# First stage of a hybrid decoder step: latents, rotary keys and p turned in 32x32 blocks on VectorE and stored in pieces of 128 bytes

## The chip, the cores and the metric

The kernel runs on one core of one Trainium2 chip. The metric is the device time of one execution in microseconds, the median of several runs. Beside the timed runs there is one profiled execution, from which the trace and the profile page come. In names of engines, PE is TensorE, DVE is VectorE, ACT is ScalarE, POOL is GpSimd and SP is SyncE, which issues nearly all DMAs here.

## The reference

One layer of a decoder with two token mixers side by side, on 1024 prompt tokens and on 8 sequences of 4 sampled tokens (32 rows). What matters here is the head of the layer and what it hands to later stages:

```python
z = rmsnorm(x, ln_w) @ w_in
rq, rk, rv, rg, cq, ckv, kr, mg, ga, gb = jnp.split(z, ...)   # cq 384, ckv 256, kr 64 columns
q = (rmsnorm(cq, q_norm_w) @ w_uq)...
ckv = rmsnorm(ckv, kv_norm_w)
kr = rope(kr, pos)
...
sc = einsum('bqhd,bkhd->bhqk', qn, k_nope) + einsum('bqhr,bkr->bhqk', qr, kr)   # MLA scores of the prompt
...
x = x + sigmoid(x @ w_ple_gate) * (p @ w_ple_proj)            # p: 256 columns per token
```

The 384 + 256 + 64 = 704 columns of cq, ckv and kr are called the latents here (NLAT). They are computed with tokens on the 128 partitions, while the matmuls that use them later need columns on the partitions and tokens along the free dimension. The same holds for p and for x. Turning them is what this document is about.

## The kernel before, in words

All matrix products of the prompt are done in three passes of float32r parts (a high and a low part of each operand), by `mac` (lines 266 to 268): three matmuls for one product. `stage` (line 240) loads a piece of a weight, POOL or ACT makes its high part (line 196 or 247) and DVE its low part (line 199, `lo_of`).

The first stage (`latents`, line 461) goes over nine tiles of tokens in the order 0, 1, 8, 2 to 7; tile 8 is the 32 sampled rows. For each it issues, in program order: `turn_tile` of the tile two places ahead (DMA of x into `xt` long before; eight TensorE transposes at line 323 into two PSUM banks, copies to `turn`, a store to the scratch `xTD`); `latent_tile` (48 matmuls with the resident weights `wlat`, two norms, the rotation of the keys by `rope_nat`, stores of ckv and of the rotary keys to the outputs and of the keys to the scratch `krD`); then, one tile later, the turn of the tile's latents: three transposes at line 404, two at line 406, copies by ACT (line 408) and DVE (line 409) into `lt`, one store to the scratch `latD` (line 410); `scale_tile` of the tile two places ahead (a transposed scale by line 350, then `xn` by lines 353 to 359); and `turn_p` (line 329), which loads 256 columns of p into `pl`, turns them by two transposes (line 323), copies them by ACT and stores them to `pTD` (line 325). All transposes of the first stage use the PSUM tag `tr`, three banks.

`beside` (line 485) lets matmuls of the gates (`fill`, their stores at line 422) run between the last three tiles. Program order is a priority; within it the tile framework orders each engine's instructions by when they come ready in its own model, and puts in all waits. Every engine, and SP's queue of DMA issues too, then runs in the order so fixed. The SBUF pool of the first stage (`p1`) is closed behind it (line 486). The pool of the next stage (`p3`) takes the same memory: its first loads (`early`, lines 526 and 529, weights of the sample queries, used at line 538) can only be issued when the last tile of `p1` has been read.

Much later, in the retention's last head (lines 1078 to 1082), the latents and the rotary keys are loaded back: `latD` row by row into five tiles, `krD` as `krN`, with tokens on the partitions. At the start of the MLA stage `rope_keys` (line 1126) turns the keys by eight transposes (line 1131) and makes `krA` and `krB`, high and low parts, each with its 64 rows twice, for the score matmuls at lines 1261 and 1262. `embedding` (line 1471) loads `pTD` near the end.

Of the kernel before, what the change touches and what calls it, by code (L numbers as in the profile page):

```python
# [9 lines left out]
F32 = mybir.dt.float32  # L10
# [9 lines left out]
P = 128  # L20
D = 1024
SEQ = 1024
# [3 lines left out]
NT = SEQ + NR  # L26
TH = NT // 3
# [8 lines left out]
ROPE = 64  # L36
QL = 384
KL = 256
PLE = 256
# [5 lines left out]
NLAT = QL + KL + ROPE  # L45
# [116 lines left out]
def decode_step(ctx: ExitStack, tc: tile.TileContext, A: dict, O: dict):  # L162
    nc = tc.nc
    pe, act, dve, pool, sp = nc.tensor, nc.scalar, nc.vector, nc.gpsimd, nc.sync
# [3 lines left out]
    dram = ctx.enter_context(tc.tile_pool(name="scratch", bufs=1, space=DRAM))  # L168
# [11 lines left out]
    def tr():  # L180
        return banks["pool"].tile([P, 512], F32, tag="tr", name="tr", bufs=3)
# [10 lines left out]
    def b32(ap):  # L192
        return ap.bitcast(F32)
# [4 lines left out]
    def lo_of(out, src, hi):  # L198
        dve.tensor_tensor(out=out, in0=src, in1=b32(hi), op=ALU.subtract)  # L199
# [9 lines left out]
    ident = C("ident")  # L209
# [7 lines left out]
    gbD = [dram.tile([P, NT], F32, tag=f"gb{f}", name=f"gb{f}") for f in range(8)]  # L217
    mgD = [dram.tile([P, NT], F32, tag=f"mg{f}", name=f"mg{f}") for f in range(8)]
    gtD, goD = ([dram.tile([P, 4, NT], F32, tag=f"{n}{h}", name=f"{n}{h}") for h in range(HR)] for n in ("gt", "go"))
    latD = dram.tile([P, 5, SEQ], F32, tag="latD", name="latD")  # L220
    xTD = dram.tile([P, 8, NT], F32, tag="xTD", name="xTD")
    pTD = dram.tile([P, 2, NT], F32, tag="pTD", name="pTD")
    krD = dram.tile([P, 8, ROPE], F32, tag="krD", name="krD")

    w_in = A["w_in"][0]

# [59 lines left out]
    p1 = ph.enter_context(tc.tile_pool(name="p1", bufs=2))  # L286
# [27 lines left out]
    def turn_input(t, src, dst, nf, by=act.copy):  # L314

        n = rows(t)
        turned = []
        for half in range(0, nf, 4):
            st = p1.tile([P, 4, P], F32, tag="turn", name="turn", bufs=4)
            w = min(4, nf - half)  # L320
            pt = tr()
            for i in range(w):
                pe.transpose(pt[:, i * P:i * P + n], src[:n, (half + i) * P:(half + i + 1) * P], ident[:n, :n])
            by(st[:, :w, :n], pt[:, :w * P].rearrange("p (a b) -> p a b", a=w)[:, :, :n])
            sp.dma_start(dst[:, half:half + w, t * P:t * P + n], st[:, :w, :n])
            turned.append(st)
        return turned

    def turn_p(t):
        n = rows(t)  # L330
        pl = p1.tile([P, PLE], F32, tag="pl", name="pl", bufs=2)
        sp.dma_start(pl[:n], A["p_prompt"][0, 0, t * P:(t + 1) * P, :] if t < 8 else A["p_sample"].rearrange("l b t c -> (l b t) c"))
        turn_input(t, pl, pTD, PLE // P)

    turned = {}

# [44 lines left out]
    def latent_tile(t):  # L381
        n = rows(t)
        pq, pk = ac(), ac()
        for ps, lo, w in ((pq, 0, QL), (pk, QL, KL + ROPE)):
            for k in range(8):
                xk = tuple(v[:, t * P:t * P + n] for v in xn[k])
                wk = tuple(v[:, lo:lo + w] for v in wlat[k])
                mac(ps[:n, :w], xk, wk, k == 0, k == 7)
        la = latS if t == 8 else p1.tile([P, NLAT], F32, tag="la", name="la", bufs=2)
        cq, kv, kr = la[:n, 0:QL], la[:n, QL:QL + KL], la[:n, QL + KL:NLAT].unsqueeze(1)  # L390
        for src, dst, w, nw in ((pq[:n, :QL], cq, QL, qnw), (pk[:n, :KL], kv, KL, kvw)):
            ss = small(p1, "ss2")
            act.activation(dst, src, AF.Square, accum_out=ss[:n])
            r = rstd_of(p1, ss, n, 1.0 / w)
            dve.scalar_tensor_tensor(out=dst, in0=src, scalar=r[:n], in1=nw[:n], op0=ALU.mult, op1=ALU.mult)
        rope_nat(kr, pk[:n, KL:KL + ROPE].unsqueeze(1), t, n, p1, 1, "kro")
        if t < 8:
            sp.dma_start(O["ckv_prompt"][0, 0, t * P:(t + 1) * P, :], kv)
            sp.dma_start(O["krope_prompt"][0, 0, t * P:(t + 1) * P, :], la[:, QL + KL:])
            sp.dma_start(krD[:, t, :], la[:, QL + KL:])  # L400
            yield
            pt, pt2 = tr(), tr()
            for i in range(3):
                pe.transpose(pt[:, i * P:(i + 1) * P], la[:, i * P:(i + 1) * P], ident)
            for i in range(2):
                pe.transpose(pt2[:, i * P:(i + 1) * P], la[:, (3 + i) * P:(4 + i) * P], ident)
            lt = p1.tile([P, 5, P], F32, tag="lt", name="lt", bufs=2)
            act.copy(lt[:, 0:3, :], pt[:, :3 * P].rearrange("p (a b) -> p a b", a=3))
            dve.tensor_copy(lt[:, 3:5, :], pt2[:, :2 * P].rearrange("p (a b) -> p a b", a=2))
            sp.dma_start(latD[:, :, t * P:(t + 1) * P], lt)  # L410
        else:
            sp.dma_start(O["ckv_sample"].rearrange("l b t c -> (l b t) c"), kv)
            sp.dma_start(O["krope_sample"].rearrange("l b t c -> (l b t) c"), la[:n, QL + KL:])
# [365 lines left out]
    qkA, qkB = slots(qk8, "qkA", 4), slots(qk8, "qkB", 4)  # L779
# [288 lines left out]
    for h in range(HR):  # L1068
        chunks = prompt_chunks(h, X)
        for cost in chunks:  # L1070
            if cost is None:
                break
        nxt = {}
        if h + 1 < HR:
            rest = (head_in(h + 1, nxt), 50.3)
        else:
            rest = (gate_tiles(C_MG, mgD, range(5, 8), AF.Silu), 31.8)
            raws = [(qkB if i < 4 else qkA)("lat", (P, SEQ), F32) for i in range(5)]
            for i, raw in enumerate(raws):
                sp.dma_start(raw, latD[:, i, :])  # L1080
            krN = qkA("krN", (P, 8, ROPE), F32)
            sp.dma_start(krN, krD)
        run(woven((chain(chunks, sample_state(h, X)), 27.9 if h + 1 < HR else 32.4), rest))
        X = nxt
    hi_by[0] = hi_pool
# [18 lines left out]
    def split(raw, hi, lo):  # L1104
        act.copy(hi, raw)
        lo_of(lo, raw, hi)
        return hi, lo
# [17 lines left out]

    def rope_keys():
        for u in range(2):
            pt = tr()
            us = slice(u * 512, (u + 1) * 512)
            for i in range(4):  # L1130
                pe.transpose(pt[:ROPE, i * P:(i + 1) * P], krN[:, 4 * u + i, :], ident)
            act.copy(krA[0:ROPE, us], pt[:ROPE])
            act.copy(krA[ROPE:P, us], pt[:ROPE])
            lo_of(krB[0:ROPE, us], pt[:ROPE], krA[0:ROPE, us])
            act.copy(krB[ROPE:P, us], b32(krB[0:ROPE, us]))
            yield 0.43

    HB = 4

# [331 lines left out]
    def embedding(j):  # L1471
        pT = [xs_("pT", (P, 2, TH)) for _ in range(2)]
        for k in range(2):
            hi, lo = (pT[k][:, i, :] for i in range(2))
            raw = xs_("pTr", (P, TH), F32)
            sp.dma_start(raw, pTD[:, k, j * TH:(j + 1) * TH])
            split(raw, hi, lo)
        return pT

# [136 lines left out]
```

## Time and profile before

| | us |
|---|---|
| median of 3 runs | 2175.15 (2174.05 to 2175.59) |
| the profiled execution's own time | 2167.49 |
| its span in the trace | 2165.7 |
| TensorE busy | 2125.3 (98%) |
| VectorE busy | 1249.4 (58%) |
| ScalarE busy | 726.9 (34%) |
| GpSimd busy | 326.4 (15%) |

The granted TensorE clock of the profiled execution is 0.998 of full speed. Line numbers in rows (L404) are those of the kernel. A row of a group reads: line, engine, operation, output <- inputs, shapes, count | busy time in us (overlaps counted once), mean ns of one | idle time of the engine just before them and what ended it. A row of the timeline reads: start and duration in us, engine, line, operation, tile names, count of merged instructions, and in brackets the idle time before it and its releaser. SPq is SP's queue of DMA issues: its durations are those of the issue, not of the transfer. A row of a tile reads: line, engine, operation, count, shortest, median and longest ns, first and last start in us. A row of waits reads: who waited, for whom, us in total, times, longest us. Rows of q1 are the DMA queue that SP feeds: packets, MB, and the time that the packets took as a share of 16 engines in that window.

### The profile page before, as it was taken

The numbers are of one execution on the slowest core, as the hardware profiler recorded it, in microseconds if no ns is written. First come the engines' busy times: TensorE is split into PE (matmuls) and PEld (weight loads), VectorE is DVE, ScalarE is ACT, GpSimd is POOL, SyncE is SP. The second block draws the span as 40 slices with busy tenths as digits, with TensorE's granted clock in tenths as the row PEclk, the third lists the DMA queues.
The fourth block names the chain that finished last, engine by engine and source line by source line (L and its number), as shares of the span: only waits on it lengthen the run. The fifth ranks groups of instructions, "written<-read, shape, count | busy, mean of one in ns | idle before, by whom it ended". The sixth has DMA issues, their size and how long they took to land.

```text
span 2165.7 us, 38482 instructions
## 1 busy us (share of the span) xinstructions
PE 2125.3 (98%) x15314; PEld 1854.5 (86%) x15314; DVE 1249.4 (58%) x2799; ACT 726.9 (34%) x1535; POOL 326.4 (15%) x519
## 2 busy tenths in 40 slices
PE   8999999999999999999999999899998999999998
PEld 7988777777777898888888787788888999999998
DVE  5524565565655447666666764777777353444465
ACT  6412222433423322222222211454556342222243
POOL 2210111111100022222222220122221000000022
PEclk9999999999999999999999999999999999999999
DMA  8557666566565321533613517110112453234243
GB/s 231 147 160 256 226 208 232 186 250 231 194 237 181 109 59 49 184 111 94 204 45 119 176 54 260 44 37 12 38 56 72 141 186 99 88 91 125 78 143 117
DMA packets 264356, 299.71 MB, mean 138 GB/s; under 512 B 26544, under 2 KB 221744, under 8 KB 260080
## 3 DMA queue, kind: packets, MB, share of 16 engines
q1 hardware_dynamic: 254960, 213.36, 31.8%
q0 software_dynamic: 9216, 83.89, 10.3%
q8 instruction: 120, 1.97, 0.4%
q14 instruction: 60, 0.49, 0.1%
HBM read 233.03 MB, written 64.17 MB: 137 GB/s over the span
## 4 chain that ended last, share of the span: by engine, by line
PE 41%; DVE 4%; issue 3%; DMA 1%; POOL 1%; ACT 1%; ACTq 0%; POOLq 0%; DVEq 0%
PE mm L266 10%; PE mm L267 10%; PE mm L268 10%; PE mm L1315 2%; PE ac L266 1%; PE ac L267 1%; PE ac L268 1%; PE tr L1301 1%; DMA out_ret_sample_dram<-st 1%; PE ac L1258 1%; PE ac L1259 1%; PE ac L1260 1%; PE ac L1262 1%; PE ac L1261 1%; ACT pr L1276 1%
## 5 line engine op out<-in xcount | busy, mean ns | idle before, releaser
L266 PE MATMUL mm<-xh,wh 128*128 128x352 f32 x1344 | 456.4, 340 | 0.8 <-ACT wh L247 0.6
L267 PE MATMUL mm<-xl,wh 128*128 128x352 f32 x1344 | 435.7, 324 | 0.0
L268 PE MATMUL mm<-xh,wl 128*128 128x352 f32 x1344 | 435.1, 324 | 0.1
L266 PEld LDWEIGHTS mm<-xh,wh 128*128 128x128 f32 x1344 | 252.7, 188 | 91.5 <-issue 78.9
L267 PEld LDWEIGHTS mm<-xl,wh 128*128 128x128 f32 x1344 | 253.9, 189 | 3.3 <-issue 1.0
L268 PEld LDWEIGHTS mm<-xh,wl 128*128 128x128 f32 x1344 | 253.6, 189 | 1.1 <-issue 0.6
L199 DVE TENSOR_TENSOR wl<-wr,wh 128x512 fp32r<-128x512 f32 (+2 forms) x251 | 175.0, 709 | 131.4 <-ACT wh L247 108.0
L247 ACT CAST wh<-wr 128x512 fp32r<-128x512 f32 x216 | 129.7, 618 | 303.3 <-PE mm L267 221.9
L662 DVE STREAM_TRANSPOSE kt<-craw 128x512 f32<-128x512 f32 x256 | 160.8, 681 | 84.4 <-PE sc L666 80.1
L421 ACT ACTIVATE gev<-mm 128x352 f32<-128x352 f32 x120 | 55.5, 463 | 239.3 <-PE mm L268 149.5
L268 PE MATMUL mm<-gh,wl 128*128 128x352 f32 x384 | 124.3, 324 | 0.0
L268 PE MATMUL mm<-mh,wl 128*128 128x352 f32 x384 | 124.3, 324 | 0.0
L266 PE MATMUL mm<-mh,wh 128*128 128x352 f32 x384 | 124.3, 324 | 0.0
L266 PE MATMUL mm<-gh,wh 128*128 128x352 f32 x384 | 124.3, 324 | 0.0
L267 PE MATMUL mm<-ml,wh 128*128 128x352 f32 x384 | 124.2, 324 | 0.0
L267 PE MATMUL mm<-gl,wh 128*128 128x352 f32 x384 | 124.1, 323 | 0.0
L266 PE MATMUL mm<-wv,xh 128*128 128x512 f32 x256 | 103.0, 402 | 0.0
L855 ACT ACTIVATE on<-ac,gb,gs 128x512 f32<-128x512 f32 (+1 forms) x36 | 28.0, 777 | 218.1 <-DVE gb L853 218.0
L267 PE MATMUL mm<-wv,xh 128*128 128x512 f32 x256 | 100.9, 394 | 0.0
L268 PE MATMUL mm<-wv,xl 128*128 128x512 f32 x256 | 100.7, 393 | 0.0
L666 PE MATMUL sc<-kt,q 32*32 32x512 f32 x2560 | 94.8, 600 | 0.1
L1546 POOL TENSOR_TENSOR xr<-x1h,x1l 128x352 f32<-128x352 f32 x24 | 27.0, 1146 | 389.4 <-DVE pT L199 311.1
(389 smaller groups left out, 4563.6 us busy)
## 6 DMA issues: line engine op xcount, KB each, us to landing
wr<-in_w_in_dram SPq DMA_DIRECT2D x144, 256.0 KB, 3.0
st<-in_state_ret_dram SPq DMA_DIRECT2D x32, 512.0 KB, 4.4
out_ret_sample_dram<-st SPq DMA_DIRECT2D x32, 512.0 KB, 4.0
wr<-in_w_ple_gate_dram SPq DMA_DIRECT2D x48, 256.0 KB, 2.8
gt<-gev SPq DMA_DIRECT2D x48, 176.0 KB, 3.5
gl<-go SPq DMA_DIRECT2D x16, 528.0 KB, 5.2
gate<-ga SPq DMA_DIRECT2D x16, 528.0 KB, 3.5
g<-gt SPq DMA_DIRECT2D x32, 256.0 KB, 3.1
```

The lines of the kernel that those rows point to most:

```text
L199: dve.tensor_tensor(out=out, in0=src, in1=b32(hi), op=ALU.subtract)
L247: hi_by[0](hi, raw)
L266: pe.matmul(out, wh, xh, start=first, stop=False)
L267: pe.matmul(out, wh, xl, start=False, stop=False)
L268: pe.matmul(out, wl, xh, start=False, stop=last)
L421: act.activation(t, ps, func)
L662: dve.transpose(kt[:, 2 * i + s].rearrange("p (n r) -> p n r", r=32), src)
L666: pe.matmul(sc[32 * v:32 * v + 32, q, :], Q["q4"][qs_, j + v // 2, 2 * (g % 2) + v % 2, :], kt[qs_, v, :], start=n == 0, stop=n == NJ // 2 ...
L855: act.activation(on[:n], po, AF.Identity, bias=nb[:n], scale=s[:n])
L1258: pe.matmul(o, qh[:, qs], kh[:, ks], start=True, stop=False)
L1315: pe.matmul(po[:, :256], v[a][w], t[:, x, 256 * a:256 * a + 256], start=j + a + part == 0, stop=False, skip_group_check=True)
L1546: pool.tensor_tensor(out=xr, in0=b32(x1[f][0][:, sl]), in1=b32(x1[f][1][:, sl]), op=ALU.add)
```

## The change

`turn_blocks` is new. One VectorE instruction turns every 32x32 block of a tile by itself: partition a + i, block b, place r of the output holds partition a + r, column 32 b + i of the input (a is 0, 32, 64 or 96). What is still missing, to bring the four groups of 32 partitions side by side as tokens, is done by the store: four DMAs, one for each group of 32 partitions, each writing for 32 partitions and all blocks a piece of 32 tokens (128 bytes). The scratch tensors get the shape [blocks, 32, tokens]. Latents and p use it; x is turned by TensorE as before. The rotary keys are now columns 640 to 703 of `latD`, so `krD` and its stores go. In the retention's last head the keys are loaded already turned, twice (`krT`), and `rope_keys` only splits them. `pl` and `tp` share three buffers where `pl` had two; the declared cost of a step of `rope_keys` goes from 0.43 to 0.1.

```diff
-    latD = dram.tile([P, 5, SEQ], F32, tag="latD", name="latD")
+    latD = dram.tile([NLAT // 32, 32, SEQ], F32, tag="latD", name="latD")
-    pTD = dram.tile([P, 2, NT], F32, tag="pTD", name="pTD")
-    krD = dram.tile([P, 8, ROPE], F32, tag="krD", name="krD")
+    pTD = dram.tile([PLE // 32, 32, NT], F32, tag="pTD", name="pTD")
...
+    def turn_blocks(dst, st, src, t, n):
+        st = st.rearrange("p (b r) -> p b r", r=32)
+        dve.transpose(st[:n], src[:n].rearrange("p (b r) -> p b r", r=32))
+        for a in range(0, n, 32):
+            sp.dma_start(dst[:, :, t * P + a:t * P + a + 32].rearrange("b i t -> i b t"), st[a:a + 32])
+
     def turn_p(t):
         n = rows(t)
-        pl = p1.tile([P, PLE], F32, tag="pl", name="pl", bufs=2)
+        pl, tp = (p1.tile([P, PLE], F32, tag="pl", name=name, bufs=3) for name in ("pl", "tp"))
         sp.dma_start(pl[:n], ...)
-        turn_input(t, pl, pTD, PLE // P)
+        turn_blocks(pTD, tp, pl, t, n)
...
             sp.dma_start(O["krope_prompt"][0, 0, t * P:(t + 1) * P, :], la[:, QL + KL:])
-            sp.dma_start(krD[:, t, :], la[:, QL + KL:])
             yield
-            pt, pt2 = tr(), tr()
-            for i in range(3):
-                pe.transpose(pt[:, i * P:(i + 1) * P], la[:, i * P:(i + 1) * P], ident)
-            for i in range(2):
-                pe.transpose(pt2[:, i * P:(i + 1) * P], la[:, (3 + i) * P:(4 + i) * P], ident)
-            lt = p1.tile([P, 5, P], F32, tag="lt", name="lt", bufs=2)
-            act.copy(lt[:, 0:3, :], pt[:, :3 * P].rearrange("p (a b) -> p a b", a=3))
-            dve.tensor_copy(lt[:, 3:5, :], pt2[:, :2 * P].rearrange("p (a b) -> p a b", a=2))
-            sp.dma_start(latD[:, :, t * P:(t + 1) * P], lt)
+            turn_blocks(latD, p1.tile([P, NLAT], F32, tag="lt", name="lt", bufs=2), la, t, P)
...
-                sp.dma_start(raw, latD[:, i, :])
-            krN = qkA("krN", (P, 8, ROPE), F32)
-            sp.dma_start(krN, krD)
+                sp.dma_start(raw, latD[4 * i:4 * i + 4].rearrange("b i t -> (b i) t"))
+            krT = qkA("krT", (P, SEQ), F32)
+            for r in range(0, P, ROPE):
+                sp.dma_start(krT[r:r + ROPE], latD[20:].rearrange("b i t -> (b i) t"))
...
     def rope_keys():
         for u in range(2):
-            pt = tr()
             us = slice(u * 512, (u + 1) * 512)
-            for i in range(4):
-                pe.transpose(pt[:ROPE, i * P:(i + 1) * P], krN[:, 4 * u + i, :], ident)
-            act.copy(krA[0:ROPE, us], pt[:ROPE])
-            act.copy(krA[ROPE:P, us], pt[:ROPE])
-            lo_of(krB[0:ROPE, us], pt[:ROPE], krA[0:ROPE, us])
-            act.copy(krB[ROPE:P, us], b32(krB[0:ROPE, us]))
-            yield 0.43
+            split(krT[:, us], krA[:, us], krB[:, us])
+            yield 0.1
...
-            sp.dma_start(raw, pTD[:, k, j * TH:(j + 1) * TH])
+            sp.dma_start(raw, pTD[4 * k:4 * k + 4, :, j * TH:(j + 1) * TH].rearrange("b i t -> (b i) t"))
```

## The prediction, made before the changed kernel ran

> **What bounds the kernel now.** I read the busy shares first, then the windows by stage, the groups of the first stage by shape, the order of single instructions around each hole in TensorE, and last the DMA rows.
>
> ```profile
> span 2165.7 us, 38482 instructions
> PE 2125.3 (98%) x15314; PEld 1854.5 (86%) x15314; DVE 1249.4 (58%) x2799; ACT 726.9 (34%) x1535; POOL 326.4 (15%) x519
> ```
> ```profile
> 17.00:62.00 45.00, 41.69 (x272) 37.55 (x272) 27.39 (x89) 26.81 (x80) 11.19 (x28) 1.00 0.82 229
> 62.00:145.00 83.00, 82.79 (x532) 81.30 (x531) 29.84 (x89) 25.95 (x75) 15.22 (x32) 1.00 0.40 117
> 145.00:165.00 20.00, 17.01 (x99) 12.23 (x98) 6.03 (x16) 4.34 (x9) 5.88 (x10) 1.00 0.92 300
> ```
>
> The columns of a window are its length, then the busy time of PE, PEld, DVE, ACT and POOL, the granted clock, the DMA share and GB/s. TensorE is busy for 2125.3 of 2165.7 us. In the stage that changes it is the bound: 82.79 of 83 us, and 41.69 of 45 before that. VectorE has 17 us free in those 45 and ScalarE 18. So a TensorE instruction that is taken away is worth its own time, and a hole in TensorE that closes is worth its length. The other engines matter only where they open a new hole.
>
> **Transposes that go.** In the first stage 24 + 16 turn the latents, 16 + 2 turn p:
>
> ```profile
> L404 PE MATMUL tr<-cst,la 128*128 128x128 f32 x24 | 3.9, 272 | 0.0
> L406 PE MATMUL tr<-cst,la 128*128 128x128 f32 x16 | 3.1, 276 | 0.0
> L323 PE MATMUL tr<-cst,pl 128*128 128x128 f32 x16 | 3.2, 283 | 0.2
> ```
> ```profile
> 44.33 0.49 PE L404 MATMUL tr<-cst,la 128*128 128x128 f32 x3
> 44.66 0.38 PE L406 MATMUL tr<-cst,la 128*128 128x128 f32 x2
> 44.88 0.39 PE L350 MATMUL tr<-cst,rs_r 128*128 128x128 f32 x2
> ...
> 45.27 0.34 PE L267 MATMUL ac<-wll,xh 128*128 128x384 f32 x1
> 45.45 0.34 PE L268 MATMUL ac<-wlh,xl 128*128 128x384 f32 x1
> ...
> 49.05 0.28 PE L323 MATMUL tr<-cst,pl 32*128 32x32 f32 x2 [1.33 <-DMA pl<-in_p_sample_dram]
> ```
>
> One takes 272 ns, but they overlap: three start at 44.33, the next two at 44.66, the next kind at 44.88, so one holds TensorE for 0.11 us. 56 x 0.11 + 0.28 (the sample's two small ones, at 49.05) = 6.4 us. The ends of the price are this and the groups' busy time with its tails, 3.9 + 3.1 + 3.2 = 10.2; I take 6.4, because TensorE's next instruction starts after the spacing, not after the tail. The Trainium skill, page "TensorE: Matmul & The Clock Gate", section "Part 4: PE-mode transpose", puts one in a kernel's context at about 275 ns; by that the term would be an estimated 16.0 us. The duration agrees (272 ns), the spacing of 0.11 us does not.
>
> **Holes around them.** The row at 49.05 shows TensorE standing 1.33 us for the sample's p to land. After the change VectorE waits there instead, and it has time. The same place costs less in each later tile:
>
> ```profile
> 65.49 0.42 PE L266 MATMUL ac<-wlh,xh 128*128 128x384 f32 x1
> 65.96 0.44 PE L323 MATMUL tr<-cst,pl 128*128 128x128 f32 x2
> 66.24 1.28 PE L323 MATMUL tr<-cst,xt 128*128 128x128 f32 x8
> ```
> ```profile
> PEld tr L323 <- ACT lt L408: 0.9, 3, 0.3
> ```
>
> A 384-column matmul is followed after 0.18 us at 45.27; here after 0.47, since the transposes of p wait for a PSUM bank that ScalarE is emptying into lt. That is 0.3 us, three times: 0.9. Three of the six bank uses per tile go (two for the latents, one for p); the other three banks' waits I leave. Together 2.2, between 0 (something else is late there) and 2.2.
>
> **The seam at 150 us.** The pool of the first stage must be free before the sample queries load their weights into the same place.
>
> ```profile
> L374 DVE TENSOR_TENSOR la<-kro,kro x8: 184/190/193, 29.1 to 132.1; 128x32 f32<-128x32 f32 x8
> L404 PE MATMUL tr<-cst,la x24: 270/272/273, 35.7 to 143.3; 128*128 128x128 f32 x24
> L410 SPq DMA_DIRECT2D latD<-lt x8: 518/519/576, 39.1 to 144.3; - x8
> ```
> ```profile
> 147.68 2.26 SPq L526 DMA_DIRECT2D early<-in_w_uq_dram  x4
> 147.75 0.26 DVE L521 COPY early<-tr 128x96 f32<-128x96 f32 x1 [3.50 <-DMA latD<-lt]
> ...
> 152.29 0.81 PE L538 MATMUL mm<-early 128*32 128x384 f32 x2 [1.05 <-ACT gev L421]
> 157.78 0.83 PE L538 MATMUL mm<-early 128*32 128x384 f32 x2 [0.94 <-DMA early<-in_w_uq_dram]
> ```
>
> The last latents are ready at 132.1, but their transposes stand behind eleven us of gate matmuls in TensorE's order and come at 143.3; the store lands at 147.7, the weights are asked for then, and TensorE stands 1.05 and 0.94 us for them. On VectorE, busy for 29.84 of the 83 us up to 145, the turn can follow at once: stores by about 136, weights asked for some 8 us earlier, before TensorE wants them. I take both holes as closed: 2.0, between 0 and 2.0.
>
> **Rotary keys.** Eight transposes go, and per half three ScalarE copies and one VectorE subtraction become one of each.
>
> ```profile
> 1358.79 1.04 PE L1131 MATMUL tr<-cst,krN 128*64 128x128 f32 x8
> ...
> 1360.11 0.35 PE L266 MATMUL ac<-wqr,lh 128*128 128x256 f32 x1 [0.28 <-POOL wqr L196]
> ```
> ```profile
> 1360.00:1370.00 10.00, 8.71 (x49) 7.25 (x50) 10.00 (x23) 7.19 (x15) 2.87 (x5) 1.00 0.31 101
> ```
>
> The transposes lie in time in which TensorE waits for POOL's weights anyway, and then VectorE (10.00 of 10) is the bound, with as many subtractions as before. Between 0 and 8 x 0.11 = 0.9; I take 0. The keys' load becomes two of 256 KB and one more issue, in the retention's last head.
>
> **What is added.** VectorE turns 128x704 and 128x256 per tile and loses a 128x256 copy:
>
> ```profile
> L662 DVE STREAM_TRANSPOSE kt<-craw x256: 658/671/714, 199.0 to 711.2; 128x512 f32<-128x512 f32 x128
> L409 DVE COPY lt<-tr x8: 418/425/425, 36.6 to 143.8; 128x256 f32<-128x256 f32 x8
> ```
>
> By width 0.92 + 0.34 - 0.42 = +0.84 us per tile, about 4 us in the 45-us window that has 17 free: nothing, while the turn isn't placed ahead of the next tile's x. If that cover went, it would be 8 x 0.84 = 6.7.
>
> Stores: 8 x 4 x 704 + 8 x 4 x 256 + 256 = 30,976 pieces of 128 B, in place of 8 x (640 + 256) = 7,168 pieces of 512 B, 256 of 128 B and 1,024 of 256 B. Two stores of the same form, of 512 pieces each, in two quiet windows, 948 to 952 us with pieces of 128 B and 958.4 to 962 with 512 B:
>
> ```profile
> q1 hardware_dynamic: 528, 0.07, 11.2%
> ```
> ```profile
> q1 hardware_dynamic: 528, 0.26, 24.2%
> ```
>
> 0.112 x 16 x 4 / 528 = 13.6 ns for a piece of 128 B, 0.242 x 16 x 3.6 / 528 = 26.4 ns for 512 B. New 30,976 x 13.6 / 16 = 26.3 us of all engines, old 11.8: +14.5. In the 45 us of the first window fall three tiles of latents and four of p: 12,544 pieces against 2,944, 10.7 - 4.9 = +5.8, share 0.82 to 0.95. Tight, not over.
>
> SP issues eight stores per tile where it had three:
>
> ```profile
> 948.11 0.56 SPq L870 DMA_DIRECT2D go<-g  x1
> ```
> ```profile
> 66.28 0.52 SPq L410 DMA_DIRECT2D latD<-lt  x1
> 67.28 0.36 SPq L398 DMA_DIRECT2D out_ckv_prompt_dram<-la  x1
> 67.73 0.52 SPq L325 DMA_DIRECT2D pTD<-turn  x1
> ...
> 76.14 0.52 SPq L410 DMA_DIRECT2D latD<-lt  x1
> ```
> ```profile
> SPq L410 <- DVE lt L409: 26.7, 6, 9.5
> ```
> ```profile
> 43.71 0.51 SPq L303 DMA_DIRECT2D xt<-in_x_prompt_dram  x1
> ...
> 55.90 1.32 PE L323 MATMUL tr<-cst,xt 128*128 128x128 f32 x8
> ```
>
> A 128-byte store takes 0.56 us to issue. Between the two latD rows the queue has 10 issues that fill 6.0 of 9.86 us. + 8 x 0.56 - 1.5 makes 9.0, with 15 gaps of 0.09 (67.64 to 67.73) 10.3, where a tile will take TensorE 9.86 - 7 x 0.11 - 0.3 = 8.8. So SP falls 1.5 us behind per tile while the tiles last. Behind it stand the x and weight loads; x is asked for 12.2 us before it is turned, seven tiles x 1.5 = 10.5 us: just covered, and a queue that waited 26.7 us for lt alone has some of that to give back, because the turn no longer waits for TensorE. I take 0; the end is rival two.
>
> **Sum.** 6.4 + 2.2 + 2.0 + 0 = 10.6 us. The profiled execution took 2167.49 (span 2165.7 and 1.8 around it) and would take 2156.9. The median of the three runs is 2175.15, 7.7 above that execution; the gain carries over: 2175.15 - 10.6 = 2164.6. With the low ends (holes stay) 6.4, so 2168.8; with the rotary keys and the tails at the high end 10.6 + 3.8 + 0.9 = 15.3, so 2159.9.
>
> **Rivals.** One: the small pieces fill the DMA engines and eat the gain. If a piece costs what one of 512 B does, 26.4 ns, the first window gets 20.7 - 4.9 = +15.8 us where 45 x 0.18 = 8.1 are free; 7.7 us late loads give 2172.3. Against it stands 13.6 ns in a quiet window; for it the share of 0.82. The Trainium skill, page "DMA: Bandwidth & Descriptors", section "Specifications", says that below 512 B a transfer leaves line rate, with a read-modify-write. The trace agrees in rate (9.4 GB/s per engine against 19.4) but not that a small piece costs more than a large one. 0.15.
>
> Two: SP's queue becomes the bound, slower. To the 1.5 us per tile come waits in order as before (26.7 us over eight tiles, 3.3): 4.8 x 7 = 33.6, less the 12.2 of lead, 21.4 late: 2164.6 + 21.4 = 2186.0. It decides from 3.3 us lost per tile ((10.6 + 12.2) / 7). For it: 10.3 against 8.8; against it: the turn comes right behind la. 0.11.
>
> Three: the change doesn't move the last store ahead, since its issue stays behind the gate stores in SP's order; the seam keeps its 2.0: 2166.6. 0.12.
>
> Four: transposes cost nearer their tails, 10.2 for 6.4, with 0.9 from the rotary keys: 2159.9. For it the groups' busy time, against it the starts. 0.05.
>
> The forecast itself 0.57, its own range 2161 to 2168. 0.2% (4.35 us) is about what a measurement of this kernel tells from no change, so faster means below 2170.8: forecast, three and four, 0.74. Same: one, 0.15. Slower: two, 0.11. From 2160 to 2173 holds forecast, one and three, 0.84.
>
> **What would show it.** No TensorE groups at L404 and L406, and 66 fewer matmuls; TensorE at 98% over the first 62 us as far as x arrives; a VectorE turn of 128x704 at about 0.92 us; packets under 512 B up by some 29,700 and the first window's DMA share below 1; the sample queries' weights asked for before 140 us and no DMA-released hole at L538. Wrong if x or weight rows show TensorE or ScalarE idle for DMA in 28 to 92 us, if the turn of 128x704 takes far over 0.92, or if the 128-byte stores take clearly over 0.56 us to issue.

## The result and the profile after

The changed kernel takes 2189.08 us (median of 5 runs, 2187.09 to 2191.89) against 2175.15 for the kernel before beside it (5 runs, 2173.47 to 2178.74): ratio 1.0064, 95% interval 1.0052 to 1.0076. It is slower by some 14 us, where 10.6 us less were forecast. The profiled execution took 2189.4 us.

The page of the changed kernel, its span, its busy times and its packets:

```profile
span 2187.6 us, 38354 instructions
PE 2125.9 (97%) x15248; PEld 1853.2 (85%) x15248; DVE 1253.5 (57%) x2808; ACT 718.4 (33%) x1514; POOL 326.3 (15%) x519
DMA packets 287539, 299.96 MB, mean 137 GB/s; under 512 B 56896, under 2 KB 244928, under 8 KB 283264
```

TensorE has the 66 matmuls less that were counted (15314 to 15248), and yet it is busy for as long as before: part of its work ran at a lower clock, and it stands longer. The windows of the first stage, in the columns explained above, say where:

```profile
17.00:62.00 45.00, 43.09 (x278) 40.02 (x277) 28.06 (x90) 23.92 (x74) 10.11 (x28) 1.00 0.69 170
62.00:145.00 83.00, 71.59 (x429) 70.47 (x428) 32.81 (x92) 20.58 (x58) 13.83 (x32) 0.92 0.51 126
145.00:165.00 20.00, 12.52 (x78) 12.23 (x76) 4.80 (x10) 2.37 (x5) 5.74 (x10) 0.90 0.68 198
```

Up to 62 us nothing is lost. From 62 to 145 TensorE was busy for 82.79 us of 83 before and is now for 71.59, at 0.92 of the clock; from 145 to 165 for 12.52 instead of 17.01. The DMA engines are not fuller in the first window, 0.69 against 0.82; in the second they are, 0.51 against 0.40, far from full. The timeline of TensorE has four holes of over 1 us behind 40 us:

```profile
81.61 0.79 PE L355 MATMUL tr<-cst,rs_r 128*128 128x128 f32 x2 [7.72 <-POOL rs_r L234]
106.28 0.66 PE L265 MATMUL mm<-xh,wh 128*128 128x352 f32 x1 [1.67 <-POOL wh L196]
109.25 0.66 PE L267 MATMUL mm<-xh,wl 128*128 128x352 f32 x1 [2.01 <-DVE wl L199]
165.20 2.59 PE L534 MATMUL mm<-early 128*32 128x384 f32 x4 [7.68 <-DMA early<-in_w_uq_dram]
```

7.72 + 1.67 + 2.01 + 7.68 = 19.1 us. The chain behind the first, from the timeline of all engines:

```profile
73.72 0.44 SPq L337 DMA_DIRECT2D pl<-in_p_prompt_dram  x1
77.93 0.45 DVE L330 STREAM_TRANSPOSE tp<-pl 128x256 f32<-128x256 f32 x1 [7.62 <-DMA pl<-in_p_prompt_dram]
78.50 0.43 DVE L432 CAST own<-pt_all 128x512 f32<-128x512 int32 x1
78.96 1.06 ACT L347 ACTIVATE xs<-xt 128x1024 f32<-128x1024 f32 x1 [4.33 <-DVE own L432]
80.20 0.73 POOL L232 TENSOR_SCALAR rs_v<-ss 128x1 f32<-128x1 f32 x3 [16.15 <-ACT xs L347]
```

VectorE stands 7.62 us in its own order for a p tile that was asked for at 73.72. Behind it stands the cast of the page table (`page_rows`, which borrows the buffers of the x squares), behind that ScalarE's squares of x, then POOL's scale, then TensorE. The seam: VectorE's turn of the last latents, and SP's queue:

```profile
122.22 0.91 DVE L330 STREAM_TRANSPOSE lt<-la 128x704 f32<-128x704 f32 x1 [6.03 <-DMA latD<-lt]
```
```profile
146.45 0.34 SPq L418 DMA_DIRECT2D ga<-gev  x1
146.83 1.09 SPq L332 DMA_DIRECT2D latD<-lt  x2
150.32 0.34 SPq L418 DMA_DIRECT2D ga<-gev  x1
150.70 1.09 SPq L332 DMA_DIRECT2D latD<-lt  x2
...
158.10 0.33 SPq L418 DMA_DIRECT2D ga<-gev  x1
158.61 2.30 SPq L522 DMA_DIRECT2D early<-in_w_uq_dram  x4
```

VectorE has turned the last latents by 123.1, but their four stores leave only from 146.83 on, two by two between gate stores, and a gate store comes every 3.9 us, since it waits for TensorE's next gate product. Two more gate stores follow. So the sample queries' weights are asked for at 158.61, not at 147.68 as before, and TensorE waits 7.68 us for them.

What the added work costs by itself is near what the prediction had. The groups of VectorE by shape in the first 200 us, and SP's issues of the latent stores (shortest, median, longest ns):

```profile
L330 DVE STREAM_TRANSPOSE lt<-la 128x704 f32<-128x704 f32 x8 | 7.2, 904 | 6.0 <-DMA latD<-lt 6.0
L330 DVE STREAM_TRANSPOSE tp<-pl 128x256 f32<-128x256 f32 x8 | 3.5, 432 | 20.9 <-DMA pl<-in_p_prompt_dram 20.9
```
```profile
L332 SPq DMA_DIRECT2D latD<-lt x32: 333/507/985, 31.3 to 151.2; - x32
```

As one mark for the first stage and the seam together I use the start of the sample queries' last product (`tr<-qlT,sel`), from the rows of the tile `qlT`. In the kernel before and in the changed one:

```profile
L583 PE MATMUL tr<-qlT,sel x16: 377/378/379, 182.2 to 188.8; 128*128 128x256 f32 x16
```
```profile
L579 PE MATMUL tr<-qlT,sel x16: 377/378/379, 196.9 to 203.5; 128*128 128x256 f32 x16
```

182.2 to 196.9: 14.7 us, about the 13.9 between the medians. What it is made of can be read from one window in each kernel, from the end of a hole of 1.9 us near 28 us, which all these kernels have, to the mark. The kernel before, the changed one, p alone and the changed kernel in another order (the last two are explained below):

```profile
27.84:182.17 154.33, 149.73 (x967) 139.34 (x968) 61.39 (x193) 56.60 (x159) 30.22 (x64) 1.00 0.61 190
```
```profile
28.03:196.88 168.85, 148.53 (x908) 138.18 (x909) 67.83 (x202) 51.14 (x142) 29.20 (x64) 0.93 0.64 173
```
```profile
28.14:179.30 151.16, 146.99 (x949) 137.38 (x950) 64.69 (x202) 53.89 (x150) 29.11 (x64) 1.00 0.65 194
```
```profile
28.26:177.84 149.58, 142.93 (x909) 134.48 (x910) 68.71 (x202) 51.08 (x142) 29.24 (x64) 0.99 0.70 196
```

TensorE stands for 168.85 - 148.53 = 20.3 us of it in place of 4.6. That is 15.7 us more, and its busy time falls by only 1.2, though 58 transposes fewer lie in it, because part of the rest ran at half the clock.

### The profile page after: what moved, and what is told of

Same layout as the page of the kernel before. It is cut to its first block, busy times and chain, and to the rows that moved or that the text cites. A ratio compares the mean times of both kernels' runs of the same rounds, so it can differ in the third digit from the quotient of the medians.

```text
span 2187.6 us, 38354 instructions
## 1 busy us (share of the span) xinstructions
PE 2125.9 (97%) x15248; PEld 1853.2 (85%) x15248; DVE 1253.5 (57%) x2808; ACT 718.4 (33%) x1514; POOL 326.3 (15%) x519
## 3 DMA queue, kind: packets, MB, share of 16 engines
q0 software_dynamic: 9216, 83.89, 10.2%
## 4 chain that ended last, share of the span: by engine, by line
PE 63%; issue 3%; DVE 3%; ACT 1%; POOL 1%; DMA 0%; ACTq 0%; POOLq 0%; DVEq 0%
PE mm L265 16%; PE mm L267 15%; PE mm L266 15%; PE ac L265 2%; PE ac L267 2%; PE ac L266 2%; PE mm L1306 2%; PE tr L1292 1%; PE sc L662 1%; PE x L693 1%; PE ac L1249 1%; PE tr L862 1%; PE ac L884 1%; PE ac L1031 1%; PE ac L1250 1%
```

## The experiments

Ratios are to the kernel before on the same chip, with 95% intervals; "mark" is the start just named, from each kernel's profiled execution. The kernel before took 2166.7 to 2167.9 us on three of the chips and 2174.5 to 2174.6 on two. Theories: the pieces of 128 bytes cost time in the DMA engines; SP's queue of eight stores per tile delays what is behind it; VectorE's wait for p; and, after the first four runs, the order of issue.

| kernel | us | ratio | interval | mark |
|---|---|---|---|---|
| latents and keys alone | 2180.04 | 1.0049 | 1.0032 to 1.0065 | 198.5 |
| p alone | 2162.50 | 0.9971 | 0.9958 to 0.9984 | 179.3 |
| one store per turn | 2161.87 | 0.9973 | 0.9962 to 0.9983 | 177.2 |
| four stores, whole rows | 2163.88 | 0.9977 | 0.9967 to 0.9987 | 178.2 |
| changed kernel, order of the one above | 2163.87 | 0.9985 | 0.9974 to 0.9996 | 177.8 |
| whole rows, order of the changed kernel | 2181.03 | 1.0063 | 1.0045 to 1.0081 | 195.9 |
| faster order up to 90 us only | 2183.48 | 1.0044 | 1.0027 to 1.0061 | 193.9 |
| faster order behind 90 us only | 2177.81 | 1.0012 | 1.0000 to 1.0023 | 185.8 |
| changed kernel again | 2189.59 | 1.0073 | 1.0056 to 1.0089 | 197.6 |
| faster order, all but TensorE | 2174.99 | 1.0006 | 0.9997 to 1.0016 | 183.0 |
| p loaded one tile ahead | 2179.03 | 1.0054 | 1.0036 to 1.0072 | 194.1 |
| page_rows later | 2186.40 | 1.0051 | 1.0031 to 1.0071 | 192.2 |
| stores first | 2188.78 | 1.0056 | 1.0034 to 1.0077 | 195.2 |
| stores first, page_rows later | 2195.58 | 1.0092 | 1.0071 to 1.0114 | 202.1 |
| both placed on load | 2164.76 | 0.9986 | 0.9976 to 0.9997 | 172.0 |
| latents placed on load | 2163.61 | 0.9979 | 0.9968 to 0.9989 | 175.1 |
| p alone, stores first | 2171.83 | 0.9981 | 0.9970 to 0.9993 | 178.7 |
| p alone again | 2165.53 | 0.9991 | 0.9980 to 1.0002 | 180.5 |

**Which part, and pieces or stores.** Latents and rotary keys alone: p's turn, scratch and store as in the kernel before.

```diff
-        turn_blocks(pTD, tp, pl, t, n)
+        turn_input(t, pl, pTD, PLE // P)
```

> Latents and rotary keys by VectorE as in the changed kernel, p turned by TensorE as before (4 of the 8 stores per tile stay four, p's become one). Queue theory (SP's eight issues per tile in one in-order queue delay what is behind them: p, weights, the last store): three stores fewer per tile, so part comes back, about 2178. Piece theory (the 128-byte pieces load the DMA engines): latents are 22,528 of 30,976 pieces, so most of the loss stays, about 2184. Wait theory (VectorE stands in its order for the p tile, 7.62 us, and behind it page_rows' cast, x squares, rs_r): VectorE no longer waits for p, the 7.72 us hole at rs_r goes, the seam's 7.68 us hole stays or not: about 2174 to 2179.

p alone: the latents' transposes, `krD` and `rope_keys` as in the kernel before.

> p by VectorE with four stores of 128-byte pieces, latents and rotary keys as in the kernel before. Queue theory: three issues more per tile than before instead of five, about 2180, with the seam's hole at the sample queries' weights still there in part. Piece theory: 8,448 small pieces only, about 2175, no hole over 2 us. Wait theory: VectorE still stands for p; the hole at rs_r stays (5 to 8 us), the seam is as before: about 2180.

One store per turn:

```diff
-        for a in range(0, n, 32):
-            sp.dma_start(dst[:, :, t * P + a:t * P + a + 32].rearrange("b i t -> i b t"), st[a:a + 32])
+            o = dst.rearrange("b i s -> b (i s)").rearrange("b (p v) -> p b v", p=P)[:, :, 32 * t:32 * t + 32]
+            sp.dma_start(o, st)
```

> Changed kernel with one store per turn in place of four, the same number and size of 128-byte pieces; the tokens land in other places of the scratch, so the latents and p read later are misplaced. Queue theory: six issues fewer per tile, two fewer than before even; the loss goes, 2165 to 2172, weights for the sample queries asked for before 150 us. Piece theory: nothing changes, about 2189. Wait theory: the p load still stands behind two stores, lands 2 to 3 us earlier, hole at rs_r about 4 us: about 2180.

Four stores of whole rows. Here, as in the version above, the later loads are left as they were, so they do not read latents and p from where these are written; only the times of the two are used:

```diff
+        o = dst.rearrange("b i s -> (b i s)").rearrange("(q c) -> q c", c=st.shape[1] * 32)
         for a in range(0, n, 32):
-            sp.dma_start(dst[:, :, t * P + a:t * P + a + 32].rearrange("b i t -> i b t"), st[a:a + 32])
+            sp.dma_start(o[t * P + a:t * P + a + 32], st[a:a + 32].rearrange("p b r -> p (b r)"))
```

> Changed kernel with its four stores per turn, but each partition's row whole (2,816 B of latents, 1 KB of p) in place of 22 and 8 pieces of 128 B; the places in the scratch are not those read later, so latents and p are misplaced. Queue theory: still eight issues per tile; if an issue's cost does not hang on its pieces, about 2189; if it does (0.33 to 0.55 us now), somewhat less, 2183. Piece theory: the small pieces are gone, 2165 to 2172. Wait theory: the p load stands behind as many stores, hole at rs_r stays at 6 to 8 us: about 2187.

Measured: 1.0049, 0.9971, 0.9973, 0.9977. Each theory is hit from one side. Fewer stores with the same pieces take the loss away, which speaks against the pieces; as many stores with no pieces take it away too, which speaks against the number of issues. p alone is faster than before, though VectorE waits for p there too (three times, 8.4 us in all, the longest 5.27), so that wait alone cannot be the whole. The changed kernel and the one with whole rows have the same instructions one for one, and only the shape of the stores differs; but the framework, which orders each engine by its own model of when things are ready, put 68 of TensorE's 13,221 in another place, 31 of VectorE's 2,598, 28 of SP's 786, 14 of ScalarE's and 4 of GpSimd's, all in the first stage and at the seam.

**The order by itself.** The instructions of one kernel, held to the order of the other by edges that carry order and no wait:

```diff
     with tile.TileContext(nc) as tc:
         decode_step(tc, A, O, **kw)
+        in_order(nc, tc)
```

First the changed kernel in the order of the one with whole rows, then the one with whole rows in the order of the changed kernel (its later loads again left as they were).

> Changed kernel with its own stores (four per turn, 128-byte pieces), but every engine and SP's queue held to the order of instructions that the kernel with whole rows got from the framework. Piece theory (the pieces cost the loss on the chip itself, in issue or in the DMA engines): it stays, 2184 to 2190. Order theory (the framework's model charges the 128-byte stores more, so it orders TensorE, VectorE and SP otherwise, and that order is what stands): the loss goes, 2161 to 2168, the holes at rs_r and at the sample queries under 4 us each.

> The other way round: whole rows in four stores per turn (latents and p read later are misplaced), every engine held to the order that the changed kernel has. Piece theory: as the kernel with whole rows, 2161 to 2168. Order theory: as the changed kernel, 2183 to 2190, with a hole of 6 us or more at rs_r and at the sample queries. If both matter, between.

0.9985 and 1.0063. The stores' shape changes nothing that can be measured at a given order (0.9985 and 0.9977 in the faster one; 1.0063 and, for the changed kernel, 1.0064 and 1.0073 in the other). The order is the cause. In the changed kernel with the other order, the windows, two of TensorE's holes, VectorE's wait for p, and SP's queue:

```profile
17.00:62.00 45.00, 43.10 (x283) 40.00 (x282) 29.46 (x93) 25.24 (x77) 12.25 (x31) 1.00 0.72 183
62.00:145.00 83.00, 78.58 (x482) 77.15 (x481) 36.43 (x100) 21.79 (x61) 17.11 (x37) 0.98 0.63 161
```
```profile
78.08 0.59 PE L355 MATMUL tr<-cst,rs_r 128*128 128x128 f32 x2 [3.28 <-POOL rs_r L234]
...
152.01 0.83 PE L534 MATMUL mm<-early 128*32 128x384 f32 x2 [1.39 <-DMA early<-in_w_uq_dram]
```
```profile
74.26 0.45 DVE L330 STREAM_TRANSPOSE tp<-pl 128x256 f32<-128x256 f32 x1 [6.64 <-DMA pl<-in_p_prompt_dram]
```
```profile
132.06 1.03 SPq L332 DMA_DIRECT2D latD<-lt  x2
133.18 0.51 SPq L418 DMA_DIRECT2D ga<-gev  x1
133.74 1.09 SPq L332 DMA_DIRECT2D latD<-lt  x2
...
141.36 2.82 SPq L522 DMA_DIRECT2D early<-in_w_uq_dram  x4
```

The same eight stores per tile, the same pieces, and the last two stores of latents go at 133.7 instead of 150.7 (VectorE turns these latents later here, at 131.12, and the stores follow at once), the weights are asked for 17 us earlier, and the hole at the scale is 3.28 us instead of 7.72. With the whole rows in the changed kernel's order the holes are back:

```profile
81.45 0.80 PE L356 MATMUL tr<-cst,rs_r 128*128 128x128 f32 x2 [7.45 <-POOL rs_r L234]
...
164.15 2.60 PE L535 MATMUL mm<-early 128*32 128x384 f32 x4 [7.35 <-DMA early<-in_w_uq_dram]
```

**Where in the order.** Both orders are cut at TensorE's 430th instruction and joined crosswise; then TensorE alone is left in the changed kernel's order.

> Changed kernel with its own stores; every engine held to the faster order (that of the kernel with whole rows) up to TensorE's 430th instruction, about 90 us, and to the changed kernel's order behind it. If the late x transposes ahead of the hole at rs_r are what costs: the first place is mended and the second (weights at 106, seam at 158 to 165) stays, 2174 to 2176, hole at rs_r about 3.5 us, hole at the sample queries 7 us or so. If the second half alone carries the loss: 2181.

> The other way round: the changed kernel's order up to TensorE's 430th instruction, the faster order behind it. By the starts of the sample queries' last product (177.8 against 195.9 us in the two orders, 6.7 of the 18.1 already there at the gates' first weights) 2169 to 2172, with the hole at rs_r of over 6 us and no hole over 2.5 us at the sample queries. If the first half alone carries the loss: 2178 or more.

> The changed kernel itself beside the others on their chip, as the mark to measure them by. At the ratio known for it (1.0064) and 2167.8 for the kernel before: 2181.6.

> Changed kernel with its own stores; TensorE held to the changed kernel's order, VectorE, ScalarE, GpSimd and SP to the faster one. If TensorE's order (x transposes 30 to 38 instructions later, the last tile's latents 165 instructions earlier) carries the loss: 2179 to 2182. If the order of SP's issues or of VectorE carries it: 2163 to 2168. TensorE's order with the others' may also wait more than either: over 2182.

On one chip: 1.0044, 1.0012, 1.0073, 1.0006. Mending the first part gains 0.29%, the second 0.61%, together 0.90%; both at once gained 0.88% (1.0073 to 0.9985, across chips). So the two places add, within the intervals. The holes at the scale and at the sample queries, with the first part mended, with the second, and with all but TensorE:

```profile
77.72 0.49 PE L355 MATMUL tr<-cst,rs_r 128*128 128x128 f32 x2 [3.28 <-POOL rs_r L234]
160.32 1.46 PE L534 MATMUL mm<-early 128*32 128x384 f32 x2 [6.87 <-DMA early<-in_w_uq_dram]
```
```profile
82.02 0.80 PE L355 MATMUL tr<-cst,rs_r 128*128 128x128 f32 x2 [7.48 <-POOL rs_r L234]
161.26 3.66 PE L534 MATMUL mm<-early 128*32 128x384 f32 x18 [1.88 <-DMA early<-in_w_uq_dram]
```
```profile
82.22 0.80 PE L355 MATMUL tr<-cst,rs_r 128*128 128x128 f32 x2 [7.16 <-POOL rs_r L234]
156.95 0.83 PE L534 MATMUL mm<-early 128*32 128x384 f32 x2 [1.32 <-DMA early<-in_w_uq_dram]
```

The hole at the scale goes with TensorE's order: in the changed kernel's, the x transposes of three tiles stand 32 to 38 instructions later. TensorE comes to this hole at about the same time in either order (73.9 in the changed kernel, 74.8 in the faster order); what differs is when the scale is ready. SP's waits between 44 and 82 us, in the changed kernel and in the faster order, show a link:

```profile
SPq L324 <- ACT turn L323: 3.3, 1, 3.3
```
```profile
SPq L324 <- ACT turn L323: 0.2, 1, 0.2
```

The store of the turned x comes later with its transposes, and SP's queue stands 3.3 us for it (3.2 with all but TensorE in the faster order). The p tile behind it is asked for at 73.72 instead of 70.31 (at 74.67 with all but TensorE), and the chain over VectorE, ScalarE and POOL starts as much later. This link is read from the traces and was not tested by itself. The hole at the seam and the late weights go with the order of the others. TensorE's order is worth 1.0006 - 0.9985 = 0.21% (across two chips, each ratio good to some 0.1%), the rest 0.67%; what of that is SP's and what VectorE's was not separated, because SP's order alone under the other engines' old one would wait for itself in a ring. I had expected TensorE's order to carry most or nothing, and it carries a quarter.

**Mending single links.** p loaded one tile ahead, in front of the stores of the tile before; page_rows three tiles later; the turns and stores marked as first in priority; the last two together.

```diff
+            if n + 1 < 9:
+                load_p(order[n + 1])
             tile_ = latent_tile(t)
...
-            if n == 4:
+            if n == 7:
                 page_rows()
...
-        dve.transpose(st[:n], ...)
+        with tc.high_priority():
+            dve.transpose(st[:n], ...)
         for a in range(0, n, 32):
+          with tc.high_priority():
             sp.dma_start(dst[:, :, t * P + a:t * P + a + 32]...
```

> Changed kernel with each p tile loaded one tile ahead in program order, ahead of the stores of the tile before, same three buffers. Wait theory (VectorE's 7.6 us for p, page_rows' cast and rs_r behind it): the hole at rs_r shrinks below 2 us and the low clock behind it goes, 2176 to 2180, the seam's hole stays. Queue or piece theory: the same stores as before stand in the queue, so 2185 to 2189. Order theory: every order is made anew, so either side is possible; the time follows the holes.

> Changed kernel with page_rows (the page table's load, cast, product and sum on VectorE, in the buffers of the x squares) three tiles later in program order. If its cast, which stands behind the p tile's turn, is the link from VectorE's wait to rs_r: the hole of 7.5 us goes below 3 us, the seam stays, ratio to the kernel before 1.0035 to 1.005 (changed kernel: 1.007). If not: hole and ratio unchanged.

> Changed kernel with the VectorE turns and their stores marked for the framework as first in priority; no order is copied. If the latent stores' place between the gate stores makes the seam late: the last one is issued before 140 us, the sample queries' weights asked for before 145, hole there under 2.5 us, at least the 0.6% of the second half come back: ratio 1.001 or below, 0.998 if the hole at rs_r goes as well. If the stores' place does not matter: 1.005 to 1.008.

> Stores first and page_rows three tiles later together. If the two links are the two halves of the loss: no hole over 3 us before 165, ratio 0.995 to 0.998, a start of the sample queries' last product at about 172 to 177 us. If page_rows is no link: as the one with the stores first.

1.0054, 1.0051, 1.0056, 1.0092. None brings it below 1.005. Each closes the hole it is aimed at, or shifts the wait, and another opens. With p ahead VectorE no longer waits 7.62 us for p but 5.11 for a buffer that p's last store still held (`pl` and `tp` share three), and TensorE's hole is 6.37:

```profile
77.88 0.45 DVE L330 STREAM_TRANSPOSE tp<-pl 128x256 f32<-128x256 f32 x1 [5.11 <-DMA pTD<-tp]
```
```profile
82.73 0.80 PE L361 MATMUL tr<-cst,rs_r 128*128 128x128 f32 x2 [6.37 <-POOL rs_r L234]
```

With page_rows later the hole at the scale is 1.16, so its cast was a link, but the gates' first weights are late; with the stores first the sample queries wait for no weights, but x and the scale come late, and a hole of 2.70 us stands behind the sample queries' first products. The largest hole ahead of the seam, with page_rows later (where the seam's own is 7.16) and then with the stores first:

```profile
102.42 0.66 PE L265 MATMUL mm<-xh,wh 128*128 128x352 f32 x1 [5.23 <-POOL wh L196]
```
```profile
89.66 0.79 PE L357 MATMUL tr<-cst,rs_r 128*128 128x128 f32 x2 [5.94 <-POOL rs_r L234]
```

I had expected the last two together to take the loss away, and they are the slowest of all. So "the last latent stores stand among the gate stores" is true of the changed kernel and not enough: of the six kernels with eight stores per tile that the framework ordered itself, five lose, and not all at the same places. Nor is it the number of stores alone: latents and keys alone, with five, lose too (1.0049), and another version with five, below, does not.

**Versions.** Both placed on load: one store of whole rows per turn, and the later loads put the 32-token pieces in place (24 loads for latents and keys, 24 for p); then the latents alone that way, with p in four stores; p alone with its stores first, and p alone once more.

```diff
-        for a in range(0, n, 32):
-            sp.dma_start(dst[:, :, t * P + a:t * P + a + 32].rearrange("b i t -> i b t"), st[a:a + 32])
+        sp.dma_start(dst[t * P:t * P + n], st[:n].rearrange("p b r -> p (b r)"))
+
+    def load_turned(out, src, b):
+        sp.dma_start(out.rearrange("i (u r) -> i u r", r=32), src[:, 32 * b:32 * b + 32].rearrange("(u i) r -> i u r", i=32))
```

> Turns by VectorE as in the changed kernel, but one store of whole rows per turn; the 128-byte pieces are put in their places by the later loads (20 for latents, 4 for the rotary keys, 24 for p, in place of 7 and 6). All theories take the loss of the first stage away: 2160 to 2168 in the first 200 us. If the loads at the retention's last head (24 issues of about 0.5 us) or at the end cost something, it shows as a hole there of some us; then up to 2172.

> Latents stored by one DMA of whole rows per tile and placed by 24 later loads of 128-byte pieces; p in four stores of pieces as in the changed kernel. Five stores per tile in place of eight. If fewer stores leave the order harmless: the sample queries' last product starts by 175 us (172 with two stores per tile, 197 in the changed kernel), and without the late p loads 2 to 4 us less than the version that placed both on load (0.9986): 0.997 to 0.998. The loads at the retention's last head still cost some 5 us there. If five stores already upset the order: 185 us or later, ratio 1.000 or more.

> Only p turned by VectorE (latents and rotary keys as in the kernel before), turn and stores put first. The version without the priority measured 0.9971. Order matters to it less, since four of eight stores per tile are not there: 0.995 to 0.998; above 0.999 would say that putting stores first takes time from x and weights.

> p alone by VectorE once more, in five rounds beside it: 0.9971 was measured, so 0.996 to 0.9985; the same order of issue as then, a start of the sample queries' last product at about 179 us.

0.9986, 0.9979, 0.9981, 0.9991. With two stores per tile the mark is at 172.0, 10.2 us before that of the kernel before. But of the 10 us only 3 arrive at the end. From the first load of the latents to the first `nm` of the MLA stage it takes 88.9 us there (1302.1 to 1391.0) against 82.6 before (1313.9 to 1396.5): the pieces now fall into the retention's last head, where the state and the next weights are loaded, and in that kernel one window there reads

```profile
1320.00:1330.00 10.00, 8.17 (x42) 7.51 (x41) 2.12 (x4) 0.93 (x2) 0.00 (x0) 0.83 1.00 272
```

a DMA share of 1.00, TensorE busy for 8.17 of 10 us, the clock at 0.83. Another 3.7 us go near the end, where p is loaded (from the first `of` to the store of the sample's output 84.8 us against 81.1 before): TensorE is busy for 19.05 us between 2080 and 2100 there, and for 20.00 with the latents alone placed on load. With five stores per tile (latents on load, p in four) the mark is at 175.1 and the ratio 0.9979, interval 0.9968 to 0.9989: faster than both kernels, than the one before by 4.5 us by the ratio and 3.0 by the medians. p alone, 0.9971 (0.9958 to 0.9984) and 0.9991 (0.9980 to 1.0002) in two measurements, is not told apart from it.

## Why the prediction was wrong, by its own steps

- **Transposes, 6.4 us.** Too small. 66 matmuls are gone, as counted. Where only p's 18 go, TensorE's busy time up to the mark falls by 149.73 - 146.99 = 2.7 us at the same clock, 0.15 us each in place of 0.11. Where 58 go, in the faster order, it falls by 6.8, and some 1.7 us of low clock stand against it (3.30 us busy at 0.50 from 78.4 to 81.7), so 8.5 is my estimate. That is between the forecast and rival four's 10.2.
- **Holes around them, 2.2.** This step failed. I moved the wait for p from TensorE to VectorE and said that VectorE has time. It has, but what stands behind the wait in its order does not: 7.62 us there became 7.72 on TensorE. The sample's hole of 1.33 is gone. Yet even in the faster order TensorE stands 6.6 us up to the mark, against 4.6 before.
- **The seam, 2.0.** This step failed, and with the wrong sign. I took the last latents' stores to follow VectorE's turn at about 136. The turn came earlier still, at 122.22, but the stores stood in SP's queue between gate stores until 151. Rival three had this mechanism, but priced it as "keeps its 2.0", as if the queue were as before; it moved the weights 11 us past the old place. Nor would the gain have come: with the weights asked for at 141.36 instead of 147.68, TensorE, earlier itself, still waits 1.39 us there.
- **SP's issues, taken as covered, 0.** This is the step that decided. I worked with a rate, 10.3 us of issues per tile against 8.8, and a lead of 12.2. (The ten issues that I put at 6.0 us fill 5.5; the eleventh belongs to the next tile.) The durations were near (median 0.51 us for a latent store, forecast 0.56), but the queue was not full: its issues between 62 and 145 us, added one by one, make 38 of 83 us in the changed kernel (82 issues) and 45 (96 issues) in the faster order. It loses time by what stands in front of what. Rival two, slower at 2186.0, came out near the measured 2189 with a chance of 0.11, but that is partly luck: for the full queue that it starts from no run speaks, and only its waits in order are what happened.
- **The framework's order, not in the sum at all.** The description of the kernel says that every engine runs in an order which the framework fixes by its own model; I never asked what order it would make of fewer transposes and more, smaller stores. 0.88% hung on it (1.0073 to 0.9985, across chips), 19 us, where my range of 2160 to 2173 was 13 us wide. With the better of two orders at hand the change would have been a gain of 0.15%, inside what I called no change. Up to the mark that order is 4.8 us shorter (149.58 for 154.33): the transposes gave some 8.5, the 4.2 for holes and seam did not come, and 2.0 of standing and 1.7 of low clock were added.
- **DMA engines, share 0.82 to 0.95.** Wrong in direction (0.69; 0.72 in the faster order), and rival one with it: at equal order pieces and whole rows are not told apart. The Trainium skill, page "DMA: Bandwidth & Descriptors", section "Specifications", puts the smallest transfer at line rate at 512 B; by that rule the 30,976 small pieces should have cost time, and in the first stage they cost none that the runs resolve. At the later loads of the version that places both on load time is lost at a share of 1.00, but there the issues are more as well as the pieces smaller, and the two were not separated. (The old 11.8 in my sum is that of the 512-byte pieces alone, without the 1,280 smaller ones.)
- **Rotary keys 0, VectorE's turning hidden.** Right. From the first cast of `few`, a tile of a later stage, to the end it takes 1428.1 us (759.5 to 2187.6) against 1428.0 (737.7 to 2165.7), so nothing is seen of the rotary keys. The turn of 128x704 takes 904 ns (forecast 0.92), that of 128x256 432 ns (forecast 0.34). It is VectorE's waiting, not its turning, that was not hidden.
- **The sum against the median.** The profiled execution of before is 7.7 us below the median, and I let the gain carry over. The stretch from the mark to the first cast of `few`, 182.2 to 737.7 in the kernel before, is 555.5 us there; it is 553 to 554 in every profile from the three chips where the kernel before takes 2167 us and 560 to 563 on the two where it takes 2174.5, also in the changed kernel's (196.9 to 759.5). So some 7 us between the two profiled executions belong to the chips and not to the change. This was read from the profiles, not tested.

## What to carry to other kernels

Where a scheduler orders the engines, a change's own instructions can be the smaller part of its price, as here: look at what order comes out, per queue, before adding up durations. Count the issues that an in-order queue gets, and ask what will stand behind each, not whether the queue has time left. When a change disappoints, hold one kernel's instructions to the other's order and the other way round; here that told what three theories by mechanism could not.

## What the runs showed of the hardware

TensorE's clock after a hole, in windows of the changed kernel around the first one and around the two shorter ones:

```profile
79.00:81.60 2.60, 0.00 (x0) 0.00 (x0) 1.34 (x2) 2.26 (x4) 1.17 (x5) 0.50 0.54 101
81.60:85.80 4.20, 4.19 (x18) 4.19 (x19) 3.70 (x15) 2.29 (x7) 2.43 (x6) 0.50 0.13 38
...
104.60:106.30 1.70, 0.03 (x2) 0.02 (x1) 0.63 (x3) 0.13 (x2) 1.40 (x4) 1.00 0.29 86
106.30:107.20 0.90, 0.90 (x2) 0.48 (x2) 0.80 (x4) 0.00 (x0) 0.51 (x1) 0.51 0.00 0
...
109.20:113.10 3.90, 3.85 (x13) 3.85 (x14) 0.59 (x1) 0.00 (x0) 0.00 (x0) 0.50 0.52 112
```

The first hole begins at 73.9; at 79.0 the granted clock is 0.50 and stays so for 4.2 us of work. After the hole of 1.67 us, and before that of 2.01, it is already 0.51, and behind the second 0.50. So a hole costs more than its length: the four holes over 1 us of the changed kernel are 19.1 us long, the two in the faster order 3.28 + 1.39 = 4.7, a difference of 14.4, while the marks differ by 196.9 - 177.8 = 19.1. For the other 4.7 us there is an estimate: TensorE was busy at about 0.50 for 4.19 + 0.90 + 3.85 us in the rows above and for 5.90 behind the seam (165.2 to 171.1), in the faster order for 3.30. If half of that is lost, it is 7.4 against 1.7, which covers them. The Trainium skill, page "TensorE: Matmul & The Clock Gate", section "Part 1: The HAM clock gate (the "warmup" mystery)", has the clock fall to half after an idle window of about 3.4 us. The 7.72 us hole agrees; the one of 1.67 us shows that less standing was enough here. The length alone does not tell it either: the hole of 1.9 us near 28 us is followed by a clock of 1.00 in the changed kernel (17 to 62 us, row further up) and of 0.88 in the version that places both on load (30 to 40 us). In latents and keys alone no hole from 62 to 145 us is longer than 2.87 us, and yet the clock is 0.88 there. My prediction priced holes at their length alone.
